# Token norms summed behind the first quarter, and the first pair's factors emitted later

## The chip, the core and the metric

The kernel runs on one core of a Trainium2 chip. The core has TensorE (PE, matmuls, with its weight loads shown as PEld), VectorE (DVE), ScalarE (ACT), GpSimd (POOL) and SyncE (SP). Matrices come from HBM by DMA, started from the queues of SP, ACT and POOL; TensorE reads SBUF and writes PSUM, which has 8 banks of 128 x 512 floats. The metric is the device time of one execution in microseconds.

## What is computed

A decoder trunk of two layers on 512 tokens of width 1024, in float32. In each layer

```
x += 1/2 * SwiGLU(RMSNorm(x))
x += Mixer(RMSNorm(x))
x += 1/2 * SwiGLU(RMSNorm(x))

RMSNorm(x, g) = x * rsqrt(mean(x*x) + 1e-6) * g
SwiGLU(x)     = (silu(x @ w_gate) * (x @ w_up)) @ w_down      # width 2816
```

The mixer of the first layer joins a pooling part and a latent attention, that of the second is a short gated convolution. So there are six norms: four ahead of feed-forward stages, two ahead of mixers. The feed-forward matrices carry most of the work.

## The kernel before

**Layout.** x lies transposed: `x[k]`, k = 0 to 7, is a tile of 128 channels by 512 tokens. Precision comes from halves: a weight chunk (128 x 1024) is split into `whi`, a cast on ScalarE (L87), and `wlo`, the rest, a subtraction on VectorE (L88); activations are split alike, and a product is three matmuls, high by high, high by low, low by high.

**Weights.** All chunks stand in one list in the order of use. `weights()` (L203) gives the next one; when it is called for chunk i it emits the split of chunk i + 2 and the loads up to chunk i + 5. The split tiles `whi` and `wlo` have three buffers each, so the split of chunk i + 3 waits until TensorE has done with chunk i.

**Norm.** When a new x[k] is final, `norm_in` emits `scaled` (xh = x times gain on ScalarE, xl, the rest, on VectorE) and `squares` (the square on ScalarE, L242, two buffers; the sum over k in `acc` by GpSimd, L247). The columns run on the unnormed xh and xl. `norm_columns` sums `acc` over the channels with four matmuls against a tile of ones (L305), makes mean plus epsilon (`nv`, L312) and its inverse root with a square root on ScalarE (L291) and small steps on VectorE (`r`). `norm_rows` spreads r over a tile `rb`, turns it with four matmuls into a PSUM bank (L320), so that all partitions hold r of each token, and copies that to SBUF as `R` (L322). In the first stage `begin` loads x and emits `scaled` and `squares` itself.

**Feed-forward stage, opening.** The products use a seven-product scheme on 2 x 2 blocks. The first pair of hidden tiles is made plainly from unnormed halves in four quarters, chunks 0 to 3, into four banks: `quarter(banks[0:2], 0)`, `quarter(banks[2:4], 0)`, then after the norm the same two for k = 4 to 7. Between the second and the third quarter the kernel emits `norm_columns`, `norm_rows` and the making of the seven factors:

```
normal(0); factor("B11"); t1 = b12 - b11; factor("T1")
normal(1); t1 -= b22;     factor("N2")
factor("B21"); t3 = b22 - b12; factor("T3"); factor("N22")
t1 = -t1 - b21;           factor("T4")
```

`normal(e)` makes four tiles xn, x times gain times R (L360). A factor is again a cast on ScalarE and a subtraction on VectorE, here over 128 x 1024. In the rows fB, fT and fN are the factors B11 and B21, T1 and T3 and T4, N2 and N22; the subtractions of t1 and t3 stand as L377, L380, L383 and, for T4, L386.

**Units.** From then on units (a gate and up pair, or half a down product) run as steps P1, P5, P6, P2, P7, P3, P4 with one chunk each, in the order that `staggered` writes out: P1, P5, P6, P2, P7 of the first unit come first. A step is 24 matmuls of 256 columns (L450). The chunk of P6 has no load of its own: it is the buffer `sto` of P5's chunk, on which GpSimd's queue adds another quarter of the weights by an accumulating DMA (L124), emitted behind P5's split and bound to both its readers. Likewise P7's chunk is P1's buffer `ar` plus a quarter. The first factor product starts when quarter four is done.

**First pair.** After quarter four the two gate products t = g R (L427), Silu (L428) and v = u R (L430) give the hidden tile, and `blocks(0, ...)` splits it into seven factors (L410 to L419 and splits) for the down products. P2's bank is the one that L427 and L430 read.

**Order of the work.** The queues of the engines are written by a planner before the run. An instruction emitted earlier goes ahead of one emitted later when both are ready on an engine; one that isn't ready is passed by. The engine then works through its queue in order.

Of the kernel before, what the change touches and what calls it, by code (L numbers as in the profile page):

```python
# [16 lines left out]
P = 128  # L17
# [24 lines left out]
def trunk(ctx: ExitStack, tc: tile.TileContext, a, out):  # L42
# [24 lines left out]
    def held():  # L67
        return bank("held", 2)
# [159 lines left out]

    class Norm:
        acc = None  # L230

    def scaled(k, which):
        g = gains[:, which, k:k + 1]
        xh = hx.tile([P, T], F32R, tag="hx", name=f"xh{k}")
        xl = hx.tile([P, T], F32R, tag="hx", name=f"xl{k}")
        nc.scalar.activation(xh, x[k], AF.Copy, scale=g)
        nc.vector.scalar_tensor_tensor(xl, x[k], g, xh.bitcast(F32), ALU.mult, ALU.subtract)  # L237
        xs[k] = (xh, xl)

    def squares(k):  # L240
        sq = tp.tile([P, T], F32, tag="sq", name="sq")
        nc.scalar.activation(sq, x[k], AF.Square)  # L242
        if k == 0:
            Norm.acc = tp.tile([P, T], F32, tag="acc", name="acc", bufs=1)
            nc.gpsimd.tensor_copy(Norm.acc, sq)
        else:
            nc.gpsimd.tensor_add(Norm.acc, Norm.acc, sq)  # L247

    def norm_in(k, which):
        scaled(k, which)  # L250
        squares(k)

    def begin():

# [47 lines left out]
    def token_sums(ps, acc):  # L302

        for i in range(NT):
            nc.tensor.matmul(ps[:, 2 * i:2 * i + 2], acc[:, i * P:(i + 1) * P], ones,  # L305
                             start=True, stop=True)

    def norm_columns():
        ps = held()
        token_sums(ps, Norm.acc)  # L310
        v = sp.tile([P, NT], F32, tag="nv", name="nv")
        nc.vector.tensor_scalar(v, ps[:, 0:2 * NT:2], 1.0 / D, EPS, ALU.mult, ALU.add)  # L312
        return rsqrt(v, NT, "n")

    def norm_rows(r):
        rb = tp.tile([P, NT, P], F32, tag="sq", name="rb")
        nc.vector.tensor_copy(rb, r.unsqueeze(2).broadcast_to([P, NT, P]))
        ps = held()
        for i in range(NT):
            nc.tensor.matmul(ps[:, i * P:(i + 1) * P], rb[:, i, :], ident, start=True, stop=True)  # L320
        R = tp.tile([P, T], F32, tag="R", name="R", bufs=1)
        nc.scalar.copy(R, ps)  # L322
        return R


    def ffn(l, f, which, after, first=False):
        what, order = plans[l, f]
        with ExitStack() as es:
# [19 lines left out]
                        mm3(ps, hi[:, s], lo[:, s], *xs[k0 + i], start and i == 0, stop and i == 3)  # L348

            quarter(banks[0:2], 0, True, False)  # L350
            quarter(banks[2:4], 0, True, False)
            r = norm_columns()
            R = norm_rows(r)
            with tc.tile_pool(name="np", bufs=1) as np_:
                xn = [np_.tile([P, 4, T], F32, tag=f"xn{e}", name=f"xn{e}") for e in range(2)]

                def normal(e):
                    for i in range(4):
                        k = 4 * e + i
                        nc.vector.scalar_tensor_tensor(xn[e][:, i], x[k], gains[:, which, k:k + 1], R,  # L360
                                                       ALU.mult, ALU.mult)

                def factor(b, v, sign=1.0):
                    hi, lo = fac[b][:, 0], fac[b][:, 1]
                    if sign > 0:
                        split(v, hi, lo)
                    else:
                        nc.scalar.mul(hi, v, -1.0)
                        nc.vector.scalar_tensor_tensor(lo, v, -1.0, hi.bitcast(F32), ALU.mult, ALU.subtract)

                normal(0)
                b11, b12 = xn[0][:, :, :HT], xn[0][:, :, HT:]
                b21, b22 = xn[1][:, :, :HT], xn[1][:, :, HT:]
                factor("B11", b11)
                hz = eight()
                t1, t3 = hz[:, :4], hz[:, 4:]
                nc.vector.tensor_sub(t1, b12, b11)  # L377
                factor("T1", t1)
                normal(1)
                nc.vector.tensor_sub(t1, t1, b22)  # L380
                factor("N2", t1)
                factor("B21", b21)
                nc.vector.tensor_sub(t3, b22, b12)  # L383
                factor("T3", t3)
                factor("N22", b22, -1.0)
                nc.vector.scalar_tensor_tensor(t1, t1, -1.0, b21, ALU.mult, ALU.subtract)  # L386
                factor("T4", t1)
# [36 lines left out]
            for e in range(2):  # L424
# [9 lines left out]
                else:  # L434
                    nc.vector.tensor_mul(hz[:, B21], v[:, :HT], t[:, :HT])
                    nc.vector.scalar_tensor_tensor(hz[:, N22], v[:, HT:], -1.0, t[:, HT:], ALU.mult, ALU.mult)
            blocks(0, hz, False)
            blocks(0, hz, True)


            live = {}
# [83 lines left out]
                    for k in range(4 * e0, 4 * e0 + 4):  # L525
                        after(k)

            for i, s in order:
                kind, p = what[i]
                (gate_up if kind == "gu" else down)(i, p, s)  # L530

# [4 lines left out]
    def even_mixer(after):  # L536
        with ExitStack() as es:
# [23 lines left out]
            with tc.tile_pool(name="ap", bufs=1) as ap:  # L561
# [16 lines left out]
                for j in range(5):  # L578
                    n = H * DQK if j < 3 else H * (DN + DV)
                    raw = raw_tile()  # L580
                    nc.sync.dma_start(out=raw[:, :n], in_=a["a_w_q_up"][j] if j < 3 else a["a_w_kv_up"][j - 3])
                    z = bank()
                    column(z, weights(), xs)
                    hi = ap.tile([P, n], F32R, tag=f"uph{j}", name=f"uph{j}")
                    lo = ap.tile([P, n], F32R, tag=f"upl{j}", name=f"upl{j}")
                    split(raw[:, :n], hi, lo)
                    wq.append((hi, lo))
                    if j == 0:
                        r = norm_columns()
                    if j == 1:  # L590
                        R = norm_rows(r)
                    zh = ap.tile([P, T], F32R, tag=f"zh{j}", name=f"zh{j}")
                    zl = ap.tile([P, T], F32R, tag=f"zl{j}", name=f"zl{j}")
                    g = lcol[:, j:j + 1]
                    nc.scalar.activation(zh, z, AF.Copy, scale=g)
                    nc.vector.scalar_tensor_tensor(zl, z, g, zh.bitcast(F32), ALU.mult, ALU.subtract)
                    lat.append((zh, zl))
                    if j in (0, 3):
                        acc = (tp if j == 0 else ap).tile([P, T], F32, tag="acc", name="lacc", bufs=1)
                        nc.scalar.activation(acc, z, AF.Square)  # L600
                        accs.append(acc)
                    else:
                        sq = tp.tile([P, T], F32, tag="sq", name="sq")
                        nc.scalar.activation(sq, z, AF.Square)
                        nc.gpsimd.tensor_add(accs[-1], accs[-1], sq)
# [299 lines left out]
    def odd_mixer(after):  # L905
        with tc.tile_pool(name="op", bufs=1) as op:
# [3 lines left out]
            for j in range(NK):  # L910
# [4 lines left out]
                hh = bank()  # L915
                column(hh, weights(), xs)
                if j == 0:
                    R = norm_rows(r)
                    R2 = op.tile([P, T], F32, tag="Rh", name="R2", bufs=1)
                    nc.vector.tensor_mul(R2, R, R)  # L920
                gb = bank()
# [99 lines left out]
```

## Time and profile before

| | us |
|---|---|
| runs: median of 3 (lowest, highest) | 1787.27 (1784.52, 1788.34) |
| the profiled execution, its own time | 1783.59 |
| its span | 1781.5 |
| PE busy | 1702.7 (96%) |
| DVE busy | 1319.5 (74%) |
| ACT busy | 905.8 (51%) |
| POOL busy | 333.9 (19%) |
| share of the chain that ended last: PE, DVE, DMA | 80%, 7%, 5% |

All rows below come from the one profiled execution; times count from the start of its span. A row of a timeline has the start, the duration, the engine, the line, the operation, output and inputs, the number of instructions merged, and in brackets the idle time before it with what ended that. Engines overlap the end of one instruction with the start of the next, so the step from start to start can be shorter than the duration. A row of the table of stages has the stretch and its length, then busy time and count of PE, PEld, DVE, ACT and POOL, then the granted TensorE clock as a share of full speed, the share of the DMA engines and GB/s. A group by line has the count after the x, busy time and mean duration behind the first bar, idle time and its releasers behind the second. Buffer numbers are left out of names, so P5's and P6's chunks are both `sto`.

### The profile page before, as it was taken

Reading aid. Unit: us, or ns where it says so; the run is one execution under the profiler, and the core shown is the slowest. Engines: PE = TensorE matmul, PEld = TensorE weight load, DVE = VectorE, ACT = ScalarE, POOL = GpSimd, SP = SyncE. Lnnn points to the kernel's source line nnn. Section 1 sums busy time; section 2 is a strip of 40 time slices with the busy share of each in tenths; the row PEclk is TensorE's granted clock in tenths of the full one; section 3 lists DMA queues with packets and bytes.
Section 4 is the critical chain, followed back from the end, with each engine's and each line's share of the span. In section 5 each row is a group of like instructions: output and inputs, shape, how many; then the busy total and the mean of one; then the engine's idle time right before and its main releaser. Section 6 shows DMA issues by size and latency. Waiting matters only on the chain.

```text
span 1781.5 us, 31291 instructions
## 1 busy us (share of the span) xinstructions
PE 1702.7 (96%) x12642; PEld 1597.9 (90%) x12642; DVE 1319.5 (74%) x1903; ACT 905.8 (51%) x1320; POOL 333.9 (19%) x371
## 2 busy tenths in 40 slices
PE   7899999999999799999998999999999989999998
PEld 5899999877788799999887999998788869999997
DVE  5877786767896877786788867867655568867866
ACT  5654654554655564554556646545322345545553
POOL 3111111234202111111131111112100211111111
PEclk8999999999999899999998999999999999999999
DMA  6699999641016598998667998995333258999985
GB/s 213 156 214 216 223 212 211 144 129 36 19 47 178 116 220 211 220 221 211 139 182 166 217 224 215 210 213 125 107 97 103 96 130 191 220 215 209 216 208 127
DMA packets 89184, 303.19 MB, mean 170 GB/s; under 512 B 10704, under 2 KB 11472, under 8 KB 89040
## 3 DMA queue, kind: packets, MB, share of 16 engines
q0 software_dynamic: 36864, 130.04, 41.5%
q1 hardware_dynamic: 50512, 169.89, 27.6%
q8 instruction: 99, 1.62, 0.4%
q10 hardware_dynamic: 1664, 1.26, 0.2%
q14 instruction: 45, 0.37, 0.1%
HBM read 299.06 MB, written 2.10 MB: 169 GB/s over the span
## 4 chain that ended last, share of the span: by engine, by line
PE 80%; DVE 7%; DMA 5%; issue 3%; ACT 2%; POOL 2%; ACTq 0%; SPq 0%; DVEq 0%; POOLq 0%
PE bank L450 59%; PE bank L215 6%; PE bank L216 6%; PE bank L217 6%; DMA sto<-in_ffn_w_down 2%; DMA sto<-in_ffn_w_gu 2%; DVE wlo L88 2%; ACT whi L87 1%; POOL acc L247 1%; DVE xn L360 1%; DVE x L520 1%; PE bank L852 0%; DVE xl L237 0%; PE held L215 0%; PE held L216 0%
## 5 line engine op out<-in xcount | busy, mean ns | idle before, releaser
L450 PE MATMUL bank<-fT,whi 128*128 128x256 f32 x1920 | 334.7, 277 | 3.9 <-ACT whi L87 3.4
L87 ACT CAST whi<-sto 128x1024 fp32r<-128x1024 f32 (+1 forms) x192 | 196.4, 1023 | 274.3 <-PE bank L450 133.7
L450 PE MATMUL bank<-hh,whi 128*128 128x256 f32 x1056 | 296.6, 282 | 12.5 <-ACT whi L87 7.7
L450 PE MATMUL bank<-hl,whi 128*128 128x256 f32 x1056 | 294.3, 279 | 1.8 <-DVE hl L88 1.8
L88 DVE TENSOR_TENSOR wlo<-sto,whi 128x1024 fp32r<-128x1024 f32 (+1 forms) x192 | 232.0, 1208 | 86.1 <-ACT whi L87 83.6
L450 PEld LDWEIGHTS bank<-fT,whi 128*128 128x128 f32 x1920 | 290.2, 188 | 6.0 <-ACT whi L87 4.1
L450 PE MATMUL bank<-hh,wlo 128*128 128x256 f32 x1056 | 293.6, 279 | 0.0
L450 PE MATMUL bank<-fT,wlo 128*128 128x256 f32 x960 | 265.9, 277 | 1.2 <-DVE wlo L88 1.1
L450 PE MATMUL bank<-fN,whi 128*128 128x256 f32 x1280 | 234.5, 286 | 17.1 <-ACT whi L87 14.9
L450 PE MATMUL bank<-fB,whi 128*128 128x256 f32 x1280 | 229.3, 279 | 3.3 <-DVE t L427 3.3
L450 PEld LDWEIGHTS bank<-fN,whi 128*128 128x128 f32 x1280 | 199.5, 194 | 24.2 <-ACT whi L87 15.7
L450 PEld LDWEIGHTS bank<-hh,whi 128*128 128x128 f32 x1056 | 198.2, 188 | 16.8 <-ACT whi L87 10.1
L87 ACT CAST whi<-a 128x1024 fp32r<-128x1024 f32 (+1 forms) x128 | 131.1, 1024 | 144.8 <-issue 81.6
L450 PEld LDWEIGHTS bank<-fB,whi 128*128 128x128 f32 x1280 | 196.9, 189 | 4.5 <-ACT whi L87 4.2
L450 PEld LDWEIGHTS bank<-hl,whi 128*128 128x128 f32 x1056 | 198.5, 188 | 2.6 <-DVE hl L88 2.6
L124 POOL DMA_DIRECT2D sto<-in_ffn_w_gu x120 | 104.8, 875 | 508.6 <-DVE wlo L88 358.4
L450 PEld LDWEIGHTS bank<-hh,wlo 128*128 128x128 f32 x1056 | 198.3, 188 | 0.0
L450 PE MATMUL bank<-fN,wlo 128*128 128x256 f32 x640 | 181.5, 284 | 12.3 <-DVE wlo L88 12.3
L88 DVE TENSOR_TENSOR wlo<-a,whi 128x1024 fp32r<-128x1024 f32 (+1 forms) x128 | 152.3, 1190 | 53.5 <-ACT whi L87 53.5
L88 DVE TENSOR_TENSOR wlo<-ar,whi 128x1024 fp32r<-128x1024 f32 (+1 forms) x128 | 153.7, 1201 | 46.8 <-ACT whi L87 42.3
L87 ACT CAST whi<-ar 128x1024 fp32r<-128x1024 f32 (+1 forms) x128 | 130.7, 1021 | 112.6 <-PE bank L450 51.0
L450 PEld LDWEIGHTS bank<-fT,wlo 128*128 128x128 f32 x960 | 180.2, 188 | 1.8 <-DVE wlo L88 1.8
(247 smaller groups left out, 3435.8 us busy)
## 6 DMA issues: line engine op xcount, KB each, us to landing
sto<-in_ffn_w_gu POOLq DMA_DIRECT2D x120, 512.0 KB, 7.6
a<-in_ffn_w_gu SPq DMA_DIRECT2D x80, 512.0 KB, 6.5
sto<-in_ffn_w_down POOLq DMA_DIRECT2D x48, 512.0 KB, 7.7
ar<-in_ffn_w_gu SPq DMA_DIRECT2D x40, 512.0 KB, 4.9
sto<-in_ffn_w_gu SPq DMA_DIRECT2D x40, 512.0 KB, 4.7
ar<-in_ffn_w_gu POOLq DMA_DIRECT2D x40, 512.0 KB, 5.4
a<-in_ffn_w_down SPq DMA_DIRECT2D x32, 512.0 KB, 5.9
raw<-in_c_w_in SPq DMA_DIRECT2D x24, 512.0 KB, 3.4
```

The lines of the kernel that those rows point to most:

```text
L87: nc.scalar.copy(hi, raw)
L88: nc.vector.tensor_sub(lo, raw, hi.bitcast(F32))
L124: nc.gpsimd.dma_start(out=self.unit[tag], in_=self.srcs[q], accum_op=ALU.add)
L215: nc.tensor.matmul(ps, wh, ah, start=start, stop=False)
L216: nc.tensor.matmul(ps, wh, al, start=False, stop=False)
L217: nc.tensor.matmul(ps, wl, ah, start=False, stop=stop)
L247: nc.gpsimd.tensor_add(Norm.acc, Norm.acc, sq)
L360: nc.vector.scalar_tensor_tensor(xn[e][:, i], x[k], gains[:, which, k:k + 1], R, ALU.mult, ALU.mult)
L450: nc.tensor.matmul(o, w_[:, s], a_, start=fresh and e == 0 and k == 0 and i == 0, stop=last and i == 2, skip_group_check=True)
L520: nc.vector.scalar_tensor_tensor(o, v, 0.5 * sign, o, ALU.mult, ALU.add)
```

## The change

It has four parts. In `squares` the last two squares of a norm (k = 6 and 7) are no longer added by GpSimd but kept; `norm_columns` sums three parts (acc and the two squares) with twelve matmuls into the same bank. This holds in all six norms. In a feed-forward stage `norm_columns` and `norm_rows` are emitted behind the first quarter instead of the second, and the first four xn read the bank that the row matmuls wrote (`Rp`) instead of the copy R. In `norm_in` the square of a tile is emitted ahead of its scaled halves, and at k = 4 a square root of a constant, one column wide, ahead of both; `begin` has no such root. The factors of the first pair, `blocks(0, ...)`, are emitted ahead of the fourth step of the list (P2 of the first unit) instead of ahead of the first.

```diff
     class Norm:
         acc = None
+        late = []
...
     def squares(k):
         sq = tp.tile([P, T], F32, tag="sq", name="sq")
         nc.scalar.activation(sq, x[k], AF.Square)
-        if k == 0:
+        if k >= NK - 2:
+            Norm.late.append(sq)
+        elif k == 0:
...
     def norm_in(k, which):
+        if k == 4:
+
+            d = sp.tile([P, 1], F32, tag="nvs", name="d")
+            nc.scalar.activation(d, eps, AF.Sqrt)
+        squares(k)
         scaled(k, which)
-        squares(k)
...
     def norm_columns():
+
         ps = held()
-        token_sums(ps, Norm.acc)
+        parts = [Norm.acc, *Norm.late]
+        Norm.late.clear()
+        for j, acc in enumerate(parts):
+            for i in range(NT):
+                nc.tensor.matmul(ps[:, 2 * i:2 * i + 2], acc[:, i * P:(i + 1) * P], ones,
+                                 start=i + j == 0, stop=j == len(parts) - 1, skip_group_check=True)
...
-        return R
+        return R, ps
...
             quarter(banks[0:2], 0, True, False)
+            r = norm_columns()
+            R, Rp = norm_rows(r)
             quarter(banks[2:4], 0, True, False)
-            r = norm_columns()
-            R = norm_rows(r)
...
-                        nc.vector.scalar_tensor_tensor(xn[e][:, i], x[k], gains[:, which, k:k + 1], R,
+                        nc.vector.scalar_tensor_tensor(xn[e][:, i], x[k], gains[:, which, k:k + 1], R if e else Rp,
...
-            blocks(0, hz, False)
-            blocks(0, hz, True)
...
-            for i, s in order:
+            for n, (i, s) in enumerate(order):
+                if n == 3:
+                    blocks(0, hz, False)
+                    blocks(0, hz, True)
                 kind, p = what[i]
...
-                        R = norm_rows(r)
+                        R, _ = norm_rows(r)
```

The second call in the odd mixer changes in the same way as the last hunk.

## Rows read from the trace of the kernel before

**Rows 1.** The page, busy time, share of the span and instructions of each engine.

```profile
PE 1702.7 (96%) x12642; PEld 1597.9 (90%) x12642; DVE 1319.5 (74%) x1903; ACT 905.8 (51%) x1320; POOL 333.9 (19%) x371
```

**Rows 2.** Groups by line, whole span: shape, count, busy, mean, idle, releaser.

```profile
L450 PE MATMUL bank<-fN,whi 128*128 128x256 f32 x1280 | 234.5, 286 | 17.1 <-ACT whi L87 14.9
...
L450 PE MATMUL bank<-fN,wlo 128*128 128x256 f32 x640 | 181.5, 284 | 12.3 <-DVE wlo L88 12.3
...
L216 PE MATMUL bank<-xl,whi 128*128 128x512 f32 x392 | 156.2, 399 | 3.8 <-DVE xl L237 3.8
...
L247 POOL TENSOR_TENSOR acc<-acc,sq 128x512 f32<-128x512 f32 x42 | 68.8, 1637 | 62.2 <-ACT sq L242 60.8
```

**Rows 3.** Timeline, TensorE, first units: start us, duration us, instruction, [idle before, releaser].

```profile
51.17 0.50 PE L450 MATMUL bank<-fN,whi 128*128 128x256 f32 x2 [1.67 <-ACT whi L87]
...
1454.79 0.40 PE L450 MATMUL bank<-fB,whi 128*128 128x256 f32 x2
...
1465.37 0.50 PE L450 MATMUL bank<-fN,whi 128*128 128x256 f32 x2 [4.49 <-ACT whi L87]
...
1470.60 0.58 PE L450 MATMUL bank<-fN,wlo 128*128 128x256 f32 x1 [3.10 <-DVE wlo L88]
...
1478.43 0.39 PE L450 MATMUL bank<-fT,whi 128*128 128x256 f32 x2
...
1485.10 0.50 PE L450 MATMUL bank<-fT,whi 128*128 128x256 f32 x2 [0.84 <-ACT whi L87]
```

**Rows 4.** Table of stages, last feed-forward opening: two stretches, all engines, clock, DMA.

```profile
1442.00:1448.00 6.00, 6.00 (x36) 5.18 (x36) 2.50 (x8) 1.76 (x3) 1.09 (x1) 1.00 1.00 214
...
1471.00:1474.00 3.00, 3.00 (x16) 3.00 (x16) 3.00 (x6) 0.63 (x1) 0.88 (x1) 0.50 0.45 56
```

**Rows 5.** Timeline, TensorE, token sums, the next quarter, row matmuls, last opening.

```profile
1442.05 0.95 PE L305 MATMUL held<-ones,acc 128*128 128x2 f32 x8
...
1442.86 0.49 PE L215 MATMUL bank<-xh,whi 128*128 128x512 f32 x1
...
1446.40 1.05 PE L320 MATMUL held<-ident,rb 128*128 128x128 f32 x8
```

**Rows 6.** Timeline, VectorE, last opening.

```profile
1443.14 1.23 DVE L88 TENSOR_TENSOR wlo<-ar,whi 128x1024 fp32r<-128x1024 f32 x1
...
1448.11 3.40 DVE L360 SCALAR_TENSOR_TENSOR xn<-x,gains,R 128x512 f32<-128x512 f32 x5 [2.33 <-ACT R L322]
...
1456.83 1.22 DVE L88 TENSOR_TENSOR wlo<-sto,whi 128x1024 fp32r<-128x1024 f32 x1
...
1464.77 1.22 DVE L386 SCALAR_TENSOR_TENSOR hz<-hz,xn 128x1024 f32<-128x1024 f32 x1
```

**Rows 7.** Timeline, ScalarE, last opening.

```profile
1436.58 1.05 ACT L87 CAST whi<-raw 128x1024 fp32r<-128x1024 f32 x1 [3.28 <-PE bank L216]
...
1449.37 1.05 ACT L87 CAST whi<-sto 128x1024 fp32r<-128x1024 f32 x1 [1.29 <-PE bank L216]
...
1464.27 1.05 ACT L87 CAST whi<-sto 128x1024 fp32r<-128x1024 f32 x1 [1.74 <-DMA sto<-in_ffn_w_gu]
```

**Rows 8.** Timeline, GpSimd, last opening: the addition onto P5's buffer.

```profile
1458.69 0.89 POOL L124 DMA_DIRECT2D sto<-in_ffn_w_gu  x1 [12.83 <-ACT fB L87]
```

**Rows 9.** Timeline, TensorE, token sums in the even mixer.

```profile
370.47 1.83 PE L305 MATMUL held<-ones,acc 128*128 128x2 f32 x8 [0.40 <-POOL acc L247]
```

**Rows 10.** Timeline, VectorE, ahead of the even mixer.

```profile
363.43 0.74 DVE L237 SCALAR_TENSOR_TENSOR xl<-x,gains,xh 128x512 fp32r<-128x512 f32 x1
...
364.84 4.44 DVE L237 SCALAR_TENSOR_TENSOR xl<-x,gains,xh 128x512 fp32r<-128x512 f32 x3
```

**Rows 11.** Timeline, ScalarE, a table load and its user, first stage.

```profile
53.98 1.28 ACT L428 ACT_TABLE_LOAD   x1
...
55.27 0.63 ACT L428 ACTIVATE t<-t 128x512 f32<-128x512 f32 x1
```

**Rows 12.** Timeline, TensorE, first reader of pair factors, last stage.

```profile
1541.40 0.28 PE L450 MATMUL bank<-hh,whi 128*128 128x256 f32 x1
```

More of the change, by code (lines that the diff above doesn't have):

```diff
@@ L917, in odd_mixer @@
                 if j == 0:
-                    R = norm_rows(r)
+                    R, _ = norm_rows(r)
                     R2 = op.tile([P, T], F32, tag="Rh", name="R2", bufs=1)
```

## The prediction

> **What bounds the kernel now.** I read the page's shares first, then the groups by line, then the timelines of the last feed-forward opening (1431 to 1485 us) engine by engine, and the table of stages for the clock. TensorE is busy for 96% of the span [rows 1], so time can come only from its few holes and from stretches at the low clock. The groups by line say where the holes are: in the first unit of the feed-forward stages PE waits 14.9 us for a high half, mostly of P6's weights, and 12.3 us for its low half, together 27.2 us over four stages [rows 2]. The timeline shows one of them: P1 starts at 1454.79, P6 comes 4.49 us late at 1465.37, its low half late again at 1470.60, and P7 follows at 1478.43 [rows 3]. The openings near 562 and 910 us are alike; in the first stage the hole before P6 is only 1.67 us [rows 3]. In the last opening the granted clock behind these waits is 0.50, the 1.2 GHz level, while 1.00 stands before [rows 4].
>
> What makes P6 late is a chain. The first quarter ends at 1436.58, when its weight slot is free again [rows 7]. Sums, root and rows give R, and the first xn starts at 1448.11, 11.5 us later [rows 6]. From there VectorE runs without a hole worth naming. P5's low half, `wlo<-sto`, could be made from about 1450.4 (its high half is cast at 1449.37) but runs at 1456.83, 8.7 us after the first xn, behind everything of the factors that was ready [rows 6, 7]. Only then may POOL add the next quarter onto the same buffer: issue at 1458.69, cast possible at 1464.27 after 1.74 us of waiting for the transfer, P6 at 1465.37 [rows 3, 7, 8]. From the start of P5's low half to P6 it is 8.5 us.
>
> **Sums.** Four matmuls appear as 8 passes, 0.81 us from the first to the next quarter's matmul at the full clock [rows 5], 0.10 us a pass; after waits, in the even mixer, 8 passes take 1.83 us [rows 9]. Eight more matmuls are 16 passes: 1.6 us of PE a norm, 3.7 at worst, six times. A page of the Trainium skill, FP8 and Floating Point Precision (TensorE Precision Notes), counts four passes for true FP32; the rows hold two per matmul, and by the page's count the added time would be 3.2 us a norm. The two additions that go are 1.64 us of POOL each [rows 2]; in the feed-forward stages after a mixer they were done long before.
>
> **The moved norm.** With the sums at the end of the first quarter the path to the first xn is: 24 passes, 2.4; then 3.5 from the last pass to the row matmuls (1442.86 to 1446.40) [rows 5], less about 0.8 because P1's low half (1.23 us, 1443.14) [rows 6] no longer sits between the scale and the reciprocal (it can't, its slot is freed by the second quarter); then 1.7 to the first xn, less the 0.6 of the copy of R, which the first four xn read past. Sum 6.2 us, against 11.5: xn starts 5.3 us earlier. PE reaches the end of the fourth quarter 1.6 later, at 19.8 after the first quarter's end (18.2 before: 1454.79 less 1436.58).
>
> **What is late next.** The five microseconds are worth something only if P5's low half moves with them. The order on VectorE follows the order of emission among what is ready: P5's low half had to let the whole of xn, T1 and B11 pass and got in at the one place where the next factor instruction was waiting for the xn right before it. In the changed kernel *two* low halves wait for that place. P1's, which before was made ahead of xn, now becomes ready about 3 us after xn starts, and being emitted first it takes the place. P5's then finds none until T4's subtraction is through and T4's cast is awaited: 1465.9 in the trace, 17.8 us after xn [rows 6]. So P5's low half starts at 6.2 + 17.8 = 24.0 after the first quarter's end instead of 20.3, P6 8.5 later at 32.5 instead of 28.8: **3.7 us later**, though the norm is 5.3 us earlier. What comes back: by then the factors and the gate products are done, so behind P6 only its own subtraction (1.2 us) is awaited, instead of 5.2 us from P6 to its low half (1465.37 to 1470.60) [rows 3]. That gives 4.0. The remaining matmuls up to P7 take the 7.8 us that they took, the low clock in them included, since PE again idles some 7 us. P7 comes 0.3 us earlier, and a later wait of 0.84 us for a cast, which stands behind the first pair's casts in ScalarE's order [rows 3], goes in half the cases: -0.7 us a stage. P5 itself waits too, about 2.5 us for its low half (24.0 + 1.2 against a start of P5 at 22.6), which costs nothing as P6 waits longer. Three stages: -2 (bounds -9 and +3, by the clock's phase and by whether P2 slips in front of P6).
>
> In the first stage P6 had waited only 1.67 us, not 4.49 [rows 3]. Its sums start after the fifth addition, two additions of 1.64 earlier, and take 24 passes at about 0.22 instead of 8, which cancels. R comes some 3 us earlier (an estimate: less than the 5.3 above, for these sums run at the low clock), because the row matmuls no longer stand behind the whole second quarter. From xn to P6 it is 17.8 + 8.5 = 26.3 instead of 17.3 (1465.37 less 1448.11), 9 more: P6 is 6 later, less 4.0 as above: +2. With the later cast I take +1.5 (bounds -5 and +4).
>
> **Mixers.** PE waits there for the last xl, 3.8 us in all [rows 2], and 0.4 for the last addition before the sums at 370 [rows 9]: xl takes 0.74 us alone and 1.48 beside POOL's additions [rows 10]. Two additions fewer let the last two run freely: 1.5 us each, about 3 of the 4.2, and the sums no longer wait for 3.3 us of additions, against 1.6 of passes a mixer. With the slower passes there (1.83 us for 8) I take -1 each, -2 together (bounds -6 and +4).
>
> **Root table and first pair.** The table load takes 1.28 us and the next instruction starts 0.01 us behind it [rows 11]. It needs no data, so in the changed order it would run behind the cast at the first quarter's end while the sums run: worth 0 either way. The Trainium skill's page ScalarE: Activation LUTs (What ACT_TABLE_LOAD costs) adds a drain of about 1.38 us to each switch; no such gap is in these rows, and by it an early load would save 1 us in two stages. The square put ahead of xh delays xh by its 0.6 and is hidden except in the mixers, where it is in the bounds. The first pair's factors (4 small operations, 4 subtractions and 4 casts) pass the casts, subtractions and POOL's additions for P6, P2 and P7; nothing reads them before the first down product at 1541.40 [rows 12], 63 us later: 0.
>
> **Sum.** -2 + 1.5 - 2 = -2.5 us. The profiled execution took 1783.59 (span 1781.5), so 1781.1 of it; the runs' median is 1787.27, 3.7 above it, so I forecast **1785 us**. Differences under 0.2% (3.6 us) can't be told from none.
>
> **Rivals.**
> *P5's low half gets through early* (13%). If it keeps its 8.7 us after xn, P6's data are there at 6.2 + 8.7 + 8.5 = 23.4, before PE can take it (19.8 + 5.8 = 25.6, two products at the pace of 1454.79 to 1460.7). P7 then starts at about 32 instead of 41.9. Some 9.5 in three stages and 5 in the first, with the mixers: -35, **1752 us**. For it speaks that P1 could be split elsewhere; against, that one place holds one subtraction of 1.2 us and the emission order gives it to P1.
>
> *The sums cost the clock* (14%, slower). 24 passes that move two columns each stand for 2.4 us where there were 0.8. At 1442 the clock stayed at 1.00 over 8 of them [rows 4]; the 8 at 370 took more than twice as long after short waits [rows 9]. If the clock falls behind the 24, the second quarter's matmuls that stand ahead of the row matmuls lose 1.7 us (half of a stretch like 1442.86 to 1446.40 [rows 5]), and xn, P5 and P6 with them: six norms, +10, **1795 us**. It decides from the granted clock in the 3 us behind the sums: 0.5 means this one.
>
> *The early root isn't where it is written* (7%). Its only input is a constant, so it may run far from the norm and change nothing; or it stands right before the last squares and puts 1.5 us (load and root) ahead of the last xh in both mixers: +3, **1788 us**.
>
> **Chances.** Forecast 66%, of it 25 points below 1783.7, 34 within 0.2% and 7 above 1790.8; its own range is 1778 to 1792. With the rivals (13 faster; 14 slower; 6 same and 1 slower) faster is 0.38, same 0.40, slower 0.22. The range 1768 to 1794 leaves out the first rival and half of the second.
>
> **What would show it.** In the changed trace: 24 passes before the second quarter; xn about 6 us after the first quarter's end; P1's `wlo<-ar` after the eighth xn and P5's `wlo<-sto` behind T4's subtraction; P6 about 32 us after the first quarter's end, with a wait of 4 to 5 us before it, one of 2 to 3 us inside P5, and little over 1 us from P6 to its low half. If P5's low half stands before T3's, the step that failed is the order on VectorE and the gain is tens of microseconds. If the waits lie in P5 and before P6 but P7 still starts 42 us after the first quarter, the forecast's mechanism holds.

## The result and the profile after

The changed kernel takes 1813.02 us (median of four runs, 1811.01 to 1816.66), the kernel before, timed beside it, 1785.89: ratio 1.0158, 95% interval 1.0129 to 1.0186, **28 us slower** by that ratio. The forecast was 1785, and its range ended at 1794. The profiled execution took 1814.28 us, its span is 1812.5 (1781.5 before).

The page of the changed kernel, busy time of the engines, to be held against [rows 1]:

```profile
PE 1749.0 (96%) x12738; PEld 1646.9 (91%) x12738; DVE 1326.1 (73%) x1903; ACT 907.7 (50%) x1324; POOL 308.8 (17%) x359
```

TensorE is busy 46.3 us longer with 96 matmul passes more, though these take 0.1 us each. The page's groups by line (count, busy, mean ns, idle time ahead and its releaser), against [rows 2]:

```profile
L461 PE MATMUL bank<-fT,wlo 128*128 128x256 f32 x960 | 273.2, 285 | 16.5 <-DVE wlo L88 16.5
L461 PE MATMUL bank<-fN,whi 128*128 128x256 f32 x1280 | 239.7, 288 | 9.1 <-ACT whi L87 8.9
...
L461 PE MATMUL bank<-fN,wlo 128*128 128x256 f32 x640 | 183.1, 286 | 2.5 <-DVE wlo L88 2.5
```

The wait of P6 for its high half fell from 14.9 to 8.9 us and that for its low half from 12.3 to 2.5, and 16.5 us of waiting inside P5 (fT, first unit) are new: together 27.9 us, 27.2 before. So the holes moved as forecast, and the time is elsewhere. To find where, I laid the two TensorE timelines side by side, matmul by matmul. The lag, the start of the n-th matmul after the change less that before it, grows like this (an opening runs from the first quarter through the waits of the first unit; opening 3 has the end of stage 2 in it):

| stretch | lag at its end, us | growth |
|---|---|---|
| first opening | 3.95 | +4.0 |
| units of stage 1 | 9.69 | +5.7 |
| stage end and even mixer | 7.47 | -2.2 |
| opening 2 | 7.38 | -0.1 |
| units of stage 2 | 11.56 | +4.2 |
| opening 3 | 15.31 | +3.8 |
| units of stage 3 | 22.43 | +7.1 |
| stage end and odd mixer | 25.24 | +2.8 |
| opening 4 | 26.93 | +1.7 |
| units of stage 4 | 31.05 | +4.1 |

**21 of the 31 us arise in the units**, where the change touches no instruction but the first pair's factors. Here is one and the same stretch in a table of stages (busy time and count of PE, PEld, DVE, ACT, POOL; granted clock; DMA share; GB/s), before:

```profile
150.00:200.00 50.00, 49.90 (x433) 49.70 (x433) 34.17 (x42) 24.48 (x31) 8.69 (x10) 1.00 0.94 219
```

and after:

```profile
150.00:200.00 50.00, 50.00 (x423) 49.81 (x422) 31.67 (x37) 20.98 (x24) 9.39 (x11) 1.00 0.91 208
```

TensorE waits for nothing in either, at a granted clock of 1.00, and yet starts 423 passes instead of 433. From start to start in the timelines, as a mean over a product's passes, a 128x256 pass on a factor tile takes 113 to 114 ns in most products before the change and 117 after it. This time from start to start is called the pitch below. No view names this as a wait; it shows only in counts and distances of starts.

The last opening on TensorE in the changed kernel, against [rows 3, 5]:

```profile
1461.84 0.95 PE L322 MATMUL held<-ones,acc 128*128 128x2 f32 x8
1462.64 1.93 PE L322 MATMUL held<-ones,sq 128*128 128x2 f32 x16
1469.34 1.05 PE L333 MATMUL held<-ident,rb 128*128 128x128 f32 x8
...
1483.42 0.40 PE L461 MATMUL bank<-fB,whi 128*128 128x256 f32 x2
...
1490.10 0.58 PE L461 MATMUL bank<-fT,wlo 128*128 128x256 f32 x1 [3.49 <-DVE wlo L88]
...
1497.44 0.79 PE L461 MATMUL bank<-fN,whi 128*128 128x256 f32 x2 [2.27 <-ACT whi L87]
1498.70 0.58 PE L461 MATMUL bank<-fN,wlo 128*128 128x256 f32 x1 [0.47 <-DVE wlo L88]
...
1506.11 0.40 PE L461 MATMUL bank<-fT,whi 128*128 128x256 f32 x2
```

and on VectorE, against [rows 6]:

```profile
1464.61 0.16 DVE L325 TENSOR_SCALAR nv<-held 128x4 f32<-128x4 f32 x1 [5.21 <-PE held L322]
1464.68 1.23 DVE L88 TENSOR_TENSOR wlo<-raw,whi 128x1024 fp32r<-128x1024 f32 x1
1465.83 0.17 DVE L300 RECIPROCAL r<-s 128x4 f32<-128x4 f32 x1
...
1471.05 2.72 DVE L373 SCALAR_TENSOR_TENSOR xn<-x,gains,held 128x512 f32<-128x512 f32 x4 [3.73 <-ACT R L335]
...
1479.75 1.22 DVE L88 TENSOR_TENSOR wlo<-ar,whi 128x1024 fp32r<-128x1024 f32 x1
...
1487.70 1.21 DVE L399 SCALAR_TENSOR_TENSOR hz<-hz,xn 128x1024 f32<-128x1024 f32 x1
1488.83 1.21 DVE L88 TENSOR_TENSOR wlo<-sto,whi 128x1024 fp32r<-128x1024 f32 x1
```

P5's low half stands right behind T4's subtraction, 17.78 us after the first xn; the forecast said 17.8. The copy of R, ahead of the first xn, on ScalarE:

```profile
1470.43 0.59 ACT L335 COPY R<-held 128x512 f32<-128x512 f32 x1 [5.42 <-PE held L333]
```

The clock in this opening, in the same table of stages: behind the sums, in P5, in the wait ahead of P6, and in P6.

```profile
1466.00:1468.00 2.00, 2.00 (x6) 1.56 (x5) 1.08 (x5) 0.00 (x0) 0.00 (x0) 0.50 1.02 201
1491.00:1495.00 4.00, 4.00 (x20) 3.87 (x19) 3.43 (x6) 0.92 (x2) 0.58 (x1) 0.50 0.67 113
1495.00:1499.00 4.00, 1.26 (x4) 0.80 (x4) 1.58 (x3) 2.66 (x4) 0.00 (x0) 0.50 0.10 18
1499.00:1502.00 3.00, 3.00 (x15) 3.00 (x15) 3.00 (x5) 0.80 (x1) 0.87 (x1) 0.50 0.49 59
```

These are two stretches at the 1.2 GHz level: one of 3.4 us behind the sums, and one of 13.7 us that runs from the stop in P5 through P6. Before the change there was one [rows 4], of some 10 us:

```profile
1466.00:1476.00 10.00, 6.17 (x27) 5.90 (x28) 9.00 (x15) 5.00 (x7) 0.88 (x1) 0.51 0.34 61
```

### The profile page after: what moved, and what is told of

It reads as the page before. It is cut to its first block, busy times and chain, and to the rows that moved or that the text cites. A ratio compares the mean times of both kernels' runs of the same rounds, so it can differ in the third digit from the quotient of the medians.

```text
span 1812.5 us, 31505 instructions
## 1 busy us (share of the span) xinstructions
PE 1749.0 (96%) x12738; PEld 1646.9 (91%) x12738; DVE 1326.1 (73%) x1903; ACT 907.7 (50%) x1324; POOL 308.8 (17%) x359
## 4 chain that ended last, share of the span: by engine, by line
PE 86%; DVE 6%; DMA 3%; issue 2%; ACT 2%; POOL 1%; SPq 0%; ACTq 0%; DVEq 0%; POOLq 0%
PE bank L461 63%; PE bank L215 6%; PE bank L216 6%; PE bank L217 6%; DMA sto<-in_ffn_w_down 2%; DVE wlo L88 1%; DMA sto<-in_ffn_w_gu 1%; PE held L322 1%; ACT whi L87 1%; DVE x L531 1%; DVE xn L373 1%; DVE xl L238 1%; PE bank L866 0%; PE held L215 0%; PE held L216 0%
## 5 line engine op out<-in xcount | busy, mean ns | idle before, releaser
L461 PE MATMUL bank<-fT,whi 128*128 128x256 f32 x1920 | 349.9, 283 | 0.0
L461 PEld LDWEIGHTS bank<-fT,whi 128*128 128x128 f32 x1920 | 299.7, 192 | 0.8 <-ACT x L466 0.8
L461 PE MATMUL bank<-fT,wlo 128*128 128x256 f32 x960 | 273.2, 285 | 16.5 <-DVE wlo L88 16.5
L461 PE MATMUL bank<-fN,whi 128*128 128x256 f32 x1280 | 239.7, 288 | 9.1 <-ACT whi L87 8.9
L461 PEld LDWEIGHTS bank<-fT,wlo 128*128 128x128 f32 x960 | 184.6, 192 | 17.3 <-DVE wlo L88 17.3
```

Source lines behind the costliest of these rows:

```text
L461: nc.tensor.matmul(o, w_[:, s], a_, start=fresh and e == 0 and k == 0 and i == 0, stop=last and i == 2, skip_group_check=True)
```

## Experiments

**What made the units slow.** Two theories: the order of the work (halves, blocks, DMAs beside other matmuls), or the place of the tiles. The change allocates one tile of 4 bytes a partition, `d`, under a tag of its own; three buffers of 32 bytes make 96, and everything allocated behind the small pool lies 96 bytes higher, the factors among it (byte 102816 of each partition instead of 102720 in the built programs). The first four runs move tiles and nothing else.

```
+    sp.tile([P, 1], F32, tag="pad", name="pad", bufs=1)    # e1; bufs=2 in e2; on the changed kernel in e4
     ones = const.tile([P, 2], F32, name="ones")
 ...
+            fp.tile([P, 1], F32, tag="pad2", name="pad2")  # e3: and this behind the factors
```

> The kernel before, with one tile of 4 bytes per partition that nothing writes or reads, allocated in the small pool sp: it takes 32 bytes, and every tile of the pools opened later moves up by 32 bytes; the instructions and their order are those of before. The seven factor tiles begin at byte 102752 of each partition (32 over a multiple of 64) where before has 102720 (a multiple of 64) and after 102816 (32 over). Address theory: the slow-down of the changed kernel is where its new 4-byte tile d pushed the factor tiles; 128x256 passes on them start 116.9 ns apart as in after, not 113.2, and 6720 such passes make about +25 us: 1808 to 1813. Schedule theory (the longer passes come from the moved blocks and halves): 1786, no change.

> The same tile with two buffers: all later tiles move by 64 bytes, the factors to 102784, again a multiple of 64 (and of 128, which 102720 is not). Address theory with 64 as the measure: 1786, as before. If a multiple of 128 counts: below 1786 by up to some 25 us. Any shift is bad (rival): about 1810. Schedule theory: 1786.

> The kernel before with 32 bytes ahead of the seven factor tiles and 32 more behind them: only the factor tiles lie 32 bytes off a multiple of 64; hz, x1, the weights' sums ar and sto, and the down products' slots hy are on multiples again. If the factors as moving operand are what counts: 6720 passes by 3.7 ns, 1808 to 1812. If it is the tiles that VectorE, ScalarE and the DMAs write (hz, ar, sto): 1786. Schedule theory: 1786.

> The changed kernel with one more 32-byte pad: with the 96 bytes of d's tile all later tiles are 128 bytes above their place in before, the factors on 102848, a multiple of 64; the order of all instructions is that of after. Address theory: the units' drift is gone, and what is left is the change proper: 1785 to 1790. Schedule theory: 1813 as after.

Measured: e1 1808.92 us, ratio 1.0166 [1.0148, 1.0184]; e2 1818.23, 1.0218 [1.0201, 1.0236]; e3 1808.61, 1.0161 [1.0144, 1.0179]; e4 1812.39, 1.0184 [1.0165, 1.0203]. An unused tile costs as much as the whole change, and moving the factors alone (e3) as much as moving everything behind them (e1): **the place of the factors is what made the units slow, shown**. My rule for it, a multiple of 64 bytes, fell with e2 and e4. The same stretch of the table of stages in e2 counts 418 passes, 120 ns each:

```profile
150.00:200.00 50.00, 50.00 (x418) 49.87 (x417) 32.34 (x38) 22.53 (x29) 9.60 (x11) 1.00 0.88 212
```

The next three ask what the place is measured from, and give the changed kernel its old place.

```
-            d = sp.tile([P, 1], F32, tag="nvs", name="d")              # e5, on the changed kernel
+            d = sp.tile([P, NT], F32, tag="ns", name="d")[:, :1]
 ...
+    const.tile([P, 16], F32, name="pad")                              # e6, ahead of all other tiles
 ...
+                fp.tile([P, 16], F32, tag=f"pad{b}", name="pad")      # e7, behind each factor tile
```

> The changed kernel with d in the buffers of an existing tile of the small pool (the root's own), so that no tile of a later pool moves: the factors begin at 102720 as in before. The order on every engine is that of after but for d's first place on ScalarE and eight rows in the first stage. In the run before this one 128 bytes of shift (102848, also a multiple of 64) did not bring the time back, and 64 bytes made it worse, so it is not the multiple of 64 that counts. Address theory (the place itself, whatever its rule): passes on the factors at 113.2 ns again, total 1781 to 1787. Schedule theory: 1812.

> The kernel before with 64 bytes ahead of everything: the weights' halves whi and wlo, the factors and all else move together, so each tile's own address is that of the +64 run (the factors on 102784) but its distance to whi and wlo is that of before. If the distance between moving operand and weights counts (the factors lie 64 bytes below the weights modulo 512 in before, level with them in the +64 run): 1781, no change. If the address of the moving operand alone counts: 1818.

> The kernel before with 64 bytes between one factor tile and the next: B11 stays at distance -64 to the weights (modulo 512), T1 lies at 0, N2 +64, B21 +128, T3 +192, N22 +256, T4 +320; all that follows is moved by 512. Only the pitch of the passes is read, product by product. Distance theory: P1 (B11) 113 ns a pass as in before, P5 (T1) 120 ns as in the +64 run, P6 (N2) about 117 as in the +128 run, and the rest is new: below 113 if the farthest distance is the best, with a floor at 106.7 (256 columns at 2.4 GHz). If the address's low bits do not count at all: 113 for each product.

e6 takes 1785.53 us, ratio 0.9996 [0.9983, 1.0009], and its passes are those of before:

```profile
150.00:200.00 50.00, 49.90 (x434) 49.70 (x433) 34.25 (x42) 24.11 (x31) 8.70 (x10) 1.00 0.94 222
```

So not the factors' own address counts, but **how far they lie from tiles that stayed where they were in e2 and moved along in e6**. Of what TensorE reads in the gate and up products, only the weights' halves, which it loads beside the passes, are among these. So the table below counts from them; that is by exclusion, since no run moved them alone. e7 (one execution, 1800.12) and e9, a second sweep (one execution, 1802.70), give the pitch by that distance. In e9's expectation the changed kernel stands at +96; that was a slip, its distance is +32.

> The kernel before with its seven factor tiles at other distances to the weights (modulo 512): B11 -32, T1 +96, N2 +160, B21 +224, T3 +288, N22 +352, T4 +416 (-96); all that follows is moved by 512. Read is the pitch of the passes by product. From the first sweep (-64: 114.0, 0: 119.5, +64: 117.8, +128: 118.5, +192: 115.1, +256: 119.8, +320: 117.8 ns): T1 as in after, 117; if the pitch is a smooth curve of the distance, N2 117, B21 117, N22 117, T4 115; a distance with a pitch under 113 would give a kernel faster than both.

| distance to the weights, modulo 512 bytes | ns a pass |
|---|---|
| -64 (before, e5, e6, e7) | 113.3 to 114.2 in most products (about half in e5), 117.8 in the others |
| -32 (e1, e3, e9) | 118.4 |
| 0 (e2, e7, e8) | 119.5 to 120.0 |
| +32 (changed kernel) | 116.5 to 118.0, mean 117 |
| +64 (e4, e7) | 117.8, but 113.3 in 32 of e4's 230 products |
| +96, +128, +160, +192 (e7, e9) | 120.0, 118.5, 117.6, 115.1 |
| +224, +256, +288, +320 | 118.4, 119.8, 116.9, 117.8 |
| +352, +416 | 119.9, 118.0 |

Kernels with the same distance agree, also at 64 and 576 bytes of shift (e2, e8: 120.0 both). No place under 113 was found; the kernel before stood on the best of the fifteen by chance. At it, most products run at 113.3 or at 117.8 ns throughout and change over at short waits; what picks one was not found. That goes for e5 too: 1797.87 us, ratio 1.0068 [1.0050, 1.0086], 0.9% or 16 us better than the changed kernel and 12 worse than before. Of the products without a wait at the full clock, 113 of 230 ran at 117.8 ns in e5's profiled execution and 29 of 228 in that of before, so part of e5's 12 us can be the slower rate and not the order of the work.

> The kernel before with the 16 slots hx (products of five of the pairs' blocks, and the stages' xh and xl) moved 64 bytes below the weights modulo 512, where the factors and the slots hy lie already (448 bytes ahead of hx, 64 ahead of the factors: 512 in all). Down passes on hx were 120 ns, on hy 113 to 117. Distance theory: some 1630 passes (34 of the 77 block operands, of 3696) gain up to 6.7 ns, about -8 to -11 us, and the 128x512 passes on xh and xl some more: 1770 to 1780. Address-free rival: 1786.

```
+    off = ctx.enter_context(tc.tile_pool(name="off", bufs=1))          # ahead of the pool hx
 ...
+    off.tile([P, 112], F32, tag="pad", name="pad")                     # 448 bytes
+    sp.tile([P, 16], F32, tag="pad2", name="pad2", bufs=1)             # 64 bytes
```

e10: 1780.62, ratio 0.9994 [0.9980, 1.0009]. The down passes fell from 116.4 to 113.8 ns, but the 512-column passes on xh and xl, in the same slots, rose from 227 to 233: a gain and a loss of some 7 to 10 us that cancel.

**What the order costs.** At distance 0 every product has the same 120 ns, so e8 and its variants are compared there, free of the two rates.

```
+    sp.tile([P, 1], F32, tag="pad", name="pad", bufs=15)    # e8, on the changed kernel: 96 + 480 bytes
```

> The changed kernel with 480 bytes more ahead of the factors: 576 in all, which is 64 modulo 512, so that the factors lie level with the weights' halves as in the +64 run of the kernel before (1818.2 us against 1780.9 of before on its chip, 120.0 ns a pass, with no spread between products). At this place both kernels have one and the same pass time, so the difference from the +64 run is the change of schedule alone. Prediction's sum (-2.5): 1815. Openings as the traces of after show them (+2.8 at the first, about nothing at the rest): 1819 to 1824. If the 12 us that the changed kernel lost with every tile in its old place are the schedule: 1830.

e8: 1830.47, ratio to before 1.0284 [1.0252, 1.0316]; e2, the kernel before at that place, has 1.0218. The change of order costs 12 us by these ratios, 10.6 in the two profiled executions; e5 has about the same (0.68%, e8 against e2 0.66%), but with the slower rate in it. The lag between e2 and e8 stays about flat in the units, and grows by 1.9, -0.3, 2.7 and 4.5 us at the four openings and by 0.9 and 1.2 from the ends of stages 1 and 3 through the mixers. Three runs undo one part each.

```
-        squares(k)                                  # e11
         scaled(k, which)
+        squares(k)
 ...
-        if k >= NK - 2:                             # e12: GpSimd adds all squares, 4 matmuls
-            Norm.late.append(sq)
-        elif k == 0:
+        if k == 0:
 ...
+            blocks(0, hz, False)                    # e13: ahead of unit 0, as before
+            blocks(0, hz, True)
```

> The changed kernel at the level place (e8, 1830.5 us; the kernel before there is e2, 1818.2) with one part undone: norm_in emits scaled(k) ahead of squares(k) again. In e8 each of three feed-forward stages ends with the last unit's low half 1.7 us late (hn,wlo idle 1.70 to 1.71, against 0.35 to 0.49 in e2), behind two xl on VectorE. Theory: the swap makes xh, and with it xl, a square later, and the xl then stand ahead of that low half: the idle falls back to 0.5, and the kernel is 3 to 4 us faster than e8: 1827. Rival (the wait comes from the shifted raw data or from blocks): no change, 1830.

> e8 with another part undone: GpSimd adds all eight squares, and 4 matmuls (8 passes) stand where 12 (24 passes) stood, behind the first quarter. In e8 the granted clock fell to 0.50 for 3 to 7 us right behind the 24 passes in two of the three later openings, and the first quarter's successor ended that much later. Theory: 8 passes do not bring the clock down; openings 3 and 4 win 1.5 to 4 us each, but the sums now wait for GpSimd's last adds (the four matmuls stand in TensorE's order right behind the first quarter): 1824 to 1830. Rival (the clock falls for the position, not for the number of passes): 1830 or more.

> e8 with the third part undone: the first pair's factors (blocks(0)) emitted ahead of unit 0's products again, as in before. If moving them was worth nothing: 1830. If it bought the shorter stalls behind P6 that e8 shows against e2 (the 0.82 us wait at the product after P7 is gone): 1833 to 1838. If it is part of the loss: under 1828.

e11: 1826.18, ratio 1.0255 [1.0237, 1.0273]. In e8 the last unit of stage 2 waits on TensorE for a low half

```profile
919.03 0.39 PE L462 MATMUL bank<-hn,wlo 128*128 128x256 f32 x1 [1.71 <-DVE wlo L89]
```

that stands behind two xl on VectorE:

```profile
914.48 3.03 DVE L239 SCALAR_TENSOR_TENSOR xl<-x,gains,xh 128x512 fp32r<-128x512 f32 x2
...
918.03 0.94 DVE L89 TENSOR_TENSOR wlo<-sto,whi 128x768 fp32r<-128x768 f32 x1
```

This wait is 1.70 us in stage 3 as well; in stage 1 it is 0.74, with 0.71 ahead of the high half, where e11's expectation has 1.7 in all three. In e11 no wait of 0.4 us or more is left at that matmul in any stage, and the ends of stages 1 to 3 are 1.1, 1.1 and 0.8 us shorter: the swap costs some 3 us in the traces, 4 by the medians. e12: 1825.35, ratio 1.0246 [1.0228, 1.0264], 5 us by the medians. The intervals of e11 and e12 overlap that of e8, so these sizes rest on the traces. e13: 1833.46, ratio 1.0290 [1.0268, 1.0312]: moving the blocks is no part of the loss, and whether the 3 us are a gain the intervals don't tell.

e12 also shows what stood ahead of the clock's fall. From the first quarter's start to P1 the last opening takes 23.66 us in e12, as in before, and 28.61 in e8. But in openings 2 and 3 the sums of e12 wait for GpSimd,

```profile
574.42 1.05 PE L321 MATMUL held<-ones,acc 128*128 128x2 f32 x8 [1.08 <-POOL acc L249]
```

and behind this short hole the clock falls as well (the same run, table of stages):

```profile
577.00:579.00 2.00, 2.00 (x6) 1.52 (x6) 1.17 (x5) 0.00 (x0) 1.48 (x2) 0.50 1.03 422
```

Behind 24 passes without a wait it fell in two of the three later openings of the changed kernel, of e4, e5, e8 and e11, and in all three of e13 and e14; behind the 8 passes of before, which had no wait ahead of them in these openings, in none.

**Where the early start went.** e14 gives P5's low half its early place on VectorE.

```
+    def ahead(n):
+        while len(ready) < used[0] + n:
+            ready.append(chunks[len(ready)].halves())
 ...
+                ahead(3)
                 factor("T1", t1)
+                ahead(4)
                 normal(1)
                 nc.vector.tensor_sub(t1, t1, b22)
                 factor("N2", t1)
+                ahead(5)
```

> The changed kernel with its factors on the old place (d in the root's buffers), scaled ahead of squares, and the halves of the first unit's weights emitted among the factors: P1's ahead of T1's halves, P5's behind them, P6's behind N2's. In the changed kernel PE stops 3.4 to 5.1 us inside P5 for its low half, which VectorE makes behind T4's subtraction, then runs the rest of P5 and P6 at a granted clock of 0.50, and waits 1.8 to 2.6 for P6's weights. Theory: with the halves early, P5 does not stop, P6's sum arrives a split and a transfer earlier, and each opening wins 4 to 6 us against e5 (1797.9 where before was 1787.7): 1775 to 1783, faster than both. Rival (VectorE is full in the opening, so what goes first delays something else by as much): 1790 to 1798.

**1770.89 us, ratio 0.9936 [0.9919, 0.9954], faster than both kernels.** The second opening on VectorE: the first xn and P5's low half, 7.85 us apart,

```profile
567.59 2.72 DVE L377 SCALAR_TENSOR_TENSOR xn<-x,gains,held 128x512 f32<-128x512 f32 x4 [4.18 <-ACT R L339]
...
575.44 1.22 DVE L88 TENSOR_TENSOR wlo<-sto,whi 128x1024 fp32r<-128x1024 f32 x1
```

and P6 on TensorE, 7.27 us behind P1 (10.84 before the change), with no stop in P5 and 1.45 us of waiting ahead of P6:

```profile
579.48 0.40 PE L468 MATMUL bank<-fB,whi 128*128 128x256 f32 x2
...
586.75 0.50 PE L468 MATMUL bank<-fN,whi 128*128 128x256 f32 x2 [1.45 <-ACT x L473]
```

The last two ask whether the early sums are needed at all, and whether fewer passes keep the clock.

```
-        if k >= NK - 2:        # e15, on e14
+        if k >= NK - 1:
```

> e14 (1770.9, ratio 0.9936 to before) with one late square in place of two: 8 matmuls, 16 passes, and GpSimd adds one square more (1.64 us). In e14, as in every run with 24 passes there, the granted clock is at 0.50 for some 3 us or more behind the sums in two or three of the later openings; with 8 passes and 1.1 us of waiting (e12) it fell too, without the wait it did not. If 16 passes without a wait keep the clock: each opening that fell wins 1.6 to 3 us, 1764 to 1768. If 16 still bring it down, or GpSimd is late by a microsecond again: 1770 to 1773.

> The kernel before with two things alone: the low halves of P1, P5 and P6 emitted early as in e14, and the first pair's factors (blocks) emitted in unit 0. The sums stand behind the second quarter with 4 matmuls, GpSimd adds all squares, no early root, no moved tile. If the gain of e14 is all in the early halves and the early sums only pay their passes and the clock: as fast as e14 or faster, 1763 to 1771. If the early sums are needed to give VectorE its 5 us of start: 1775 to 1782.

e15: **1767.17, ratio 0.9925 [0.9908, 0.9942]**; against e14 the intervals overlap, but behind its 16 passes the clock stays up in all three later openings, though in opening 3 TensorE waits 0.72 us for GpSimd ahead of them; here beside e14 (e15, then e14, last opening):

```profile
1427.00:1429.00 2.00, 2.00 (x10) 1.64 (x9) 1.76 (x7) 0.03 (x1) 0.77 (x1) 1.00 1.09 215
```

```profile
1429.00:1431.00 2.00, 2.00 (x7) 1.52 (x5) 1.76 (x6) 0.12 (x1) 0.60 (x1) 0.50 0.84 172
```

e16, the early halves with the sums where they were: 1781.95, ratio 1.0001 [0.9987, 1.0014]. Alone they bring nothing: the factor itself is late then, since VectorE starts later.

```profile
585.05 0.38 PE L454 MATMUL bank<-fN,whi 128*128 128x256 f32 x1 [2.84 <-ACT fN L87]
```

## Why the prediction was wrong

**The step that failed** is the 0 that the paragraph on the root table and the first pair books. The forecast asked what the root's instruction delays and not where its tile lies: the tile moved the factors 96 bytes, and 6720 passes on them, and down passes on the slots above, became 2 to 3 ns longer. That is 21 us of the profiled difference and 16 of the timed one (ratio 1.0158 against e5's 1.0068). With every tile in its place the forecast would still have missed by 14 us, part of which can be the slower rate in e5; the terms of the order below are the second thing that it had wrong.

**The early root** did not do what it says, a rival given 7%: its input is a constant, and all five copies ran at the start of the program. ScalarE, first microseconds:

```profile
2.46 0.57 ACT L256 ACTIVATE d<-eps 128x1 f32<-128x1 f32 x5
```

**Sums** (1.6 us a norm, 3.7 at worst). From the first quarter's start to P1 it is 25.43 us in opening 2, 1.8 more than before, and 27.02 and 27.04 in openings 3 and 4, where the clock fell behind the sums: 3.4 more. The rival "the sums cost the clock", with its 14%, was in place, mechanism and size (1.7 us an opening) right for two of three openings; it had been set as an alternative, while it came on top. In the three later openings that makes 8.5 us, where 4.8 were forecast. e12, whose 8 passes wait for GpSimd instead, spends 4.2 us less in the four openings than e8. Twelve matmuls are 24 passes, two each; the four per matmul of the Trainium skill's page FP8 and Floating Point Precision (TensorE Precision Notes) are not in this trace.

**The early xn.** 6.2 us after the first quarter were forecast; it is 8.1 where the clock holds (577.70 less 569.62) and 9.2 in the last opening, 11.5 before [rows 6, 7]. The chain from the sums to the row matmuls was taken 1.3 us too short (6.4 in opening 2, 5.1 forecast), and from these to xn 0.6. Neither of the two terms that the forecast took off came: in place of P1's low half that of another chunk (`wlo<-raw`, 1464.68) stands between the scale and the reciprocal, which were to come 0.8 closer, and the xn that read the bank start as the copy of R ends (1470.43 and 0.59 give 1471.02, xn at 1471.05), so its 0.6 stay. Why they wait for a copy that they do not read, no run shows.

**P5's low half** came as forecast counted from xn, 17.78 us after it and behind T4's subtraction, in all four openings; counted from the first quarter's end it is 27.0 in the last one, 24.0 forecast. With it came the waits: 3.5 us in P5 (2.5 forecast), 2.3 before P6 (4 to 5 forecast), 1.3 from P6 to its low half (1.2 forecast). P7 starts 42.7 us after the first quarter in opening 2 (41.6 forecast) and 44.3 in opening 4. What the sum missed is the clock again: it took "the low clock included" over from before, but a stop *inside* P5 lets P5's rest restart at 0.50, 20 passes in 4 us, and P6 behind its own wait as well. With the sums, that turned -0.7 an opening into -0.1, +3.8 and +1.7.

**The first rival** (P5's low half early, 13%, 1752) names what was missing. e14 builds it: 1.3% or 24 us faster than e5, the same order with the low half late (some 3 of them by the swap undone in it), where the rival had 33 against the forecast. Of the 35 us between the two profiled executions 25 lie in the openings and 9 in the units and stage ends, where e5 has the slower rate more often. The mechanism was right, and it needed a change of its own.

**Mixers** (-2). They brought -2.2 and +2.8; the sums no longer wait, but the swap of square and scale, booked as hidden, made xl late ahead of the stage's last low half (some 3 us in e11). **First stage** +1.5: +4.0, and +1.9 at a place without the two rates, within the bounds given.

## What to carry to other kernels

An added tile is not free because its instruction is: compare the addresses of what TensorE streams before and after a change, and count passes in an undisturbed stretch, since no wait shows the loss. A gain in start time passes only as far as the next thing in the in-order queue lets it; move that along in the same change (e16 alone gave nothing, the change of order alone cost 0.7%, together, in e14, they gained 0.6%). Where a stop falls decides what runs at the low clock behind it, so price a moved wait with its restart.

## What the runs showed of the hardware

- The pitch of a 128x256 matmul pass depends on the distance between the moving tile and, by exclusion, the weights loaded beside it: 113.3 to 120.0 ns at the same granted clock of 1.00, repeating at 64 and 576 bytes; moving all tiles together changes nothing (0.9996). 512-column passes prefer another distance (227 against 233 ns). The Trainium skill's page SBUF — State Buffer (SBUF: two separate sides) says that TensorE never waits on another engine at its port. Nothing here speaks against that, since it made no difference whether the tiles that the other engines write were moved by 32 bytes or by 64 (e1 against e3); but at one clock the pitch differs by 6% with where TensorE's own two operands lie. Whether they meet at the port, no run shows.
- At one distance, -64, two rates, 113.3 and 117.8 ns, held over whole units, and e4 has them at +64 too (32 of 230 products at the faster one); which one a unit gets stays open.
- The granted clock fell from 1.00 to 0.50 behind 24 passes of two columns in 16 of 21 openings (the three later ones of seven kernels), though TensorE had no hole there, and behind 8 of them with a wait of 1.1 or 1.2 us ahead (e12, twice); behind 16 in none of three (e15).
